# Strassen blocks of an up projection: high parts as one 512-column matmul, halves summed on GpSimd

## The chip, the cores and the metric

The kernel runs on one core of a Trainium2 chip. The time is device microseconds of one execution; the median of several runs is given. A profile is taken in an execution of its own, whose span is given beside the median. TensorE (PE in the profile) multiplies matrices out of SBUF into PSUM, with weight loads (PEld) beside the matmuls; VectorE (DVE), ScalarE (ACT) and GpSimd (POOL) do the rest, each with a queue that is worked off in order; SyncE (SP) and GpSimd issue DMAs.

## What is computed

Two layers of an encoder on 512 tokens of 1024 features. The part that the change touches is the gated MLP at the end of each layer:

```python
hf = rms_norm(x, ffn_norm_g[l])
u = depthwise_conv(hf @ ffn_w_up[l], ffn_conv_w[l], ffn_conv_b[l])
u_gate, u_val = u[..., :D_FF], u[..., D_FF:]
x = x + (jax.nn.silu(u_gate) * u_val) @ ffn_w_down[l]
```

`D_FF` is 2816, so there are 22 column blocks of 128 for the gate and 22 for the value. The depthwise convolution has width 3, along the tokens. All inputs are float32.

## The kernel before

**High and low halves.** Every matmul operand is kept as two float32r tiles, a rounded high part and the rest as a low part, and every product is three matmuls: high by high, high by low, low by high (`mm3`, L534). A weight tile of 128x512 is split by `w_split` (L441) or, for the Strassen blocks, by `w_form` (L467). ScalarE rounds (`A.activation`, which the profile shows at L299). The low half is made in one of two ways: a subtraction on VectorE or GpSimd (L306), or `by_transfer` (L432), in which ScalarE writes minus the high part and a DMA issued by GpSimd adds the raw weight (L438).

**The order.** The whole program is written out by hand: a planner (`Clock`, L208) keeps a simulated time for each engine, adds the cost of every operation that is issued, and decides by it when the steps of a `chain` (L258) are put into the engines' queues. What is put in first runs first, whatever the real times are. `wnext` (L516) hands out weights in the order of `units` and lets the splits run 3, 4 or 6 units ahead. PSUM has eight banks under the tags `acc` (2), `S` (1), `ST` (2), `AV` (2) and `mi` (1).

**The up projection.** The first 4 column blocks of a layer are computed as they stand (`plain`, L1678). The other 18 use Strassen's scheme (the Winograd form): the two halves of the features, the gate and the value columns, and the two halves of the tokens make a 2x2 by 2x2 product of blocks, done in 7 products instead of 8 (`product`, L1693). Each product is 4 weight columns (`q`) with three matmuls of 256 tokens. `forms` holds, for each product and `q`, the high and low half of its token operand: slices of `HH` and `HL` for the products 11, 12 and 4, of a tile `tf` for the others. The sums of weight blocks that the products need are made in `w_form` on VectorE (tiles `raw` and `s`); the forms 11, 12 and 22 are plain blocks and take `by_transfer` (tiles `fh`, `fl`; all other split weights are `wh`, `wl`).

Products share banks: 11, 2, 3 add up in one of `acc`, 1 and 4 in one of `AV`, 12 and 22 have one of `ST` each. After a product its bank is either copied aside by ScalarE (`aside`, tile `sx`) or added by VectorE to an earlier copy (`add`, tile `u`), 256 columns each time. Then both 512-token results are multiplied by the norm factor `rbc` on VectorE (`scale`), and go through the convolution (`convolve`, L1656: one pass on ScalarE, two multiply-adds on VectorE, tile `a`), Silu, gate product and split into `ah`/`al` or `act`.

**The down projection.** The column blocks come in groups of 4, 5, 5, 5 and 3. The 8 output blocks of a finished group (`down`, L1765, three matmuls of 512 per column block) are dealt out between the products of the next group, after the products named in `SPOTS`, and added to the residual `XM` by VectorE. `_ffn` (L115) writes this order down.

Of the kernel before, what the change touches and what calls it, by code (L numbers as in the profile page):

```python
# [47 lines left out]
FORMS = ("11", "12", "1", "22", "2", "4", "3")  # L48
SPOTS = ("22", "2", "4", "3")
# [11 lines left out]
C_BIAS = 0.2  # L61

# [51 lines left out]

def _ffn():  # L115

    toks, late = [], []
    for g, (c0, c1) in enumerate(_groups()):  # L120
        dealt = len(late) - (KEEP * SIZES[g - 1] if g == len(SIZES) - 1 else 0)
        for n, c in enumerate(range(c0, c1)):
            if g == 0:
                toks += [("u", c, 0), ("u", c, 1)]
                continue
            now = late[:dealt * (n + 1) // (c1 - c0) - dealt * n // (c1 - c0)]
            late = late[len(now):]
            for f in FORMS:
                toks.append(("f", c, f))
                if f in SPOTS:  # L130
                    k = SPOTS.index(f)
                    toks += now[len(now) * k // len(SPOTS):len(now) * (k + 1) // len(SPOTS)]
        late += [("d", g, m, i) for m in range(KC) for i in range(c1 - c0)]
    return toks + late


def _layer_units():

    r = _widths()
    for tok in _ffn():  # L140
        if tok[0] == "u":
            r += [("u", T), ("p", T), ("next",)]
        elif tok[0] == "f":
            r.append(tok)
        elif (tok[2] * SIZES[tok[1]] + tok[3]) % 4 == 0:
            r.append(("u" if tok[1] < len(SIZES) - 1 else "p", T))
    return r
# [60 lines left out]
class Clock:  # L208
# [5 lines left out]
    def __init__(self):  # L214
        self.now, self.n, self.heap, self.busy = 0.0, 0, [], False
        self.fin, self.free, self.ready = 0.0, {}, {}
        self.source = self.last = None

# [39 lines left out]
    def chain(self, *steps, after=0.2):  # L258

        def go(n, source=None):  # L260
            if n == len(steps):
                return
            keys, fn = steps[n] if isinstance(steps[n], tuple) else ((), steps[n])
# [15 lines left out]
class Engine:  # L279
# [13 lines left out]
    def activation(self, out, in_, func, **k):  # L293
        t = self.TABLE.get(func)
        if t and t != self.table and not (t == 2 and func is AF.Tanh and self.table == 3):
            self.table = t
            self.ck.took(self.kind, 1.28)
        self._count(out, 0.00084, 0.09 + 0.09 * (len(k) > 0))
        return self.eng.activation(out, in_, func, **k)  # L299

    def _two(self, out, *a):
        self._count(out, *((0.14, 0.1) if ALU.pow in a else (0.002145, 0.127) if self.kind == "Pool" else (0.00105, 0.07)))
# [17 lines left out]
    def tensor_copy(self, out, in_, psum=False):  # L320
        self._count(out, 0.00105 if psum else 0.00053, 0.07)
        return self.eng.tensor_copy(out, in_)  # L322
# [15 lines left out]
def trunk(ctx: ExitStack, tc: tile.TileContext, x, w, prm, gb, cst, out):  # L338
# [44 lines left out]
    def soonest(*tags):  # L383

        for t in tags:
            while not banks[t]:
                ck.pop()
        return min(tags, key=lambda t: banks[t][0])
# [52 lines left out]
    def w_split():  # L441
# [9 lines left out]
        hi, lo = halves[j] = pair(j)  # L451
        ck.fin = ck.now
# [14 lines left out]
    def w_form(j, form, pi):  # L467
# [6 lines left out]
        if form in ("11", "12", "22"):  # L474
            hi, lo = halves[j] = pair(j, True)
            by_transfer(hi[:, :T], lo[:, :T], {"11": a11, "12": a12, "22": a22}[form])
            done("w", j)
            return
        hi, lo = halves[j] = pair(j)
        if form == "2":  # L480
# [5 lines left out]
            "4": (a12, a12, s2, ALU.subtract, [("sum", pi, "2")], None),  # L486
# [17 lines left out]
        chain((keys, total), lambda: A.activation(hi[:, :T], dst, AF.Copy), low, after=0.0)  # L504

    def pick(bias, t=0.0):

        t = max(t, ck.now)
        dve, pool = (max(t, ck.free.get(e, 0.0)) for e in ("DVE", "Pool"))
        return V if dve + 0.61 + bias < pool + 1.18 else G  # L510

# [13 lines left out]
    def mm(o, lhsT, rhs, start, stop, again=False):  # L525
        PE.matmul(o, lhsT=lhsT, rhs=rhs, start=start, stop=stop, skip_group_check=again)  # L526
        n = rhs.shape[-1]
        ck.to(ck.now + (n / 2400.0 + 0.0133 if st["ffn"] else max(0.107, n / 2370.0)))
# [12 lines left out]
    HH = cp.tile([P, KC, T], F32R, tag="HH", name="HH")  # L541
    HL = cp.tile([P, KC, T], F32R, tag="HL", name="HL")
# [140 lines left out]
    def layer(l, sq, xsrc):  # L683
# [904 lines left out]
        def build_forms(q):  # L1588
# [51 lines left out]
        st["ffn"] = True  # L1640
# [15 lines left out]
        def convolve(c, part, u):  # L1656
# [3 lines left out]
                lambda: A.activation(a[:, :T], u[:, :T], AF.Identity, bias=col(PRM_B + ci),  # L1660
                                     scale=col(PRM_W1 + ci)),
                lambda: V.scalar_tensor_tensor(a[:, 1:T], u[:, 0:T - 1], col(PRM_W0 + ci), a[:, 1:T],
                                               ALU.mult, ALU.add),
                lambda: V.scalar_tensor_tensor(a[:, 0:T - 1], u[:, 1:T], col(PRM_W2 + ci), a[:, 0:T - 1],
                                               ALU.mult, ALU.add)]
# [27 lines left out]
        def product(c, name):  # L1693

            if name == "11":
                quad["u"], quad["v"] = slot("u"), slot("u")
                quad["s"] = [slot("sx") for _ in range(2)]
                quad["a"] = ps("acc")
            if name in ("12", "1", "22"):
                quad[name] = ps({"12": "ST", "1": "AV", "22": "ST"}[name])  # L1700
            if name == "2":
                need(("s1", l, c))
            if name == "4":
                need(("s5", l, c))
            if name == "3":
                need(("s2", l, c))
            bank = quad[{"11": "a", "2": "a", "3": "a", "4": "1"}.get(name, name)]
            o = bank[:, 0:256]
# [6 lines left out]
            u, v, (sa, sb) = quad["u"], quad["v"], quad["s"]  # L1715
            lo, hi = slice(0, 256), slice(256, 512)

            def aside(dst, key, tag=None):
                def go():
                    A.activation(dst, o, AF.Copy)  # L1720
                    if tag:
                        free(tag)
                    done(key, l, c)
                chain(go)

            def add(dst, other, tag=None):
                def go():
                    V.tensor_tensor(dst, o, other, ALU.add)
# [3 lines left out]

            def scale(t):
                return [([("rbc", G2)], lambda: V.tensor_tensor(t[:, :T], t[:, :T], fin["rbc"][:, :T], ALU.mult))]

            if name == "11":
                aside(sa[:, lo], "s1")
            elif name == "12":
                chain(([("s1", l, c)], add(u[:, lo], sa[:, lo], "ST")))
            elif name == "1":  # L1740
                aside(sb[:, lo], "s5")
            elif name == "22":
                aside(sb[:, hi], "s4", "ST")
            elif name == "2":
                aside(sa[:, hi], "s2")
# [19 lines left out]
        def down(g, m, i):  # L1765
            c0, c1 = groups[g]
            n, kc, ends = c1 - c0, c0 + i, g == len(groups) - 1
            b = m * n + i
# [44 lines left out]
        st["ffn"] = False  # L1813
# [62 lines left out]
def _pack_weights(i):  # L1876
    res = []
    for l in range(L):
# [34 lines left out]
        for kind, *tok in _ffn():  # L1913
# [8 lines left out]
            elif kind == "d":  # L1922
                g, m, k = tok
                c0, c1 = _groups()[g]
                if (m * (c1 - c0) + k) % 4 == 0:
                    at = [divmod(m * (c1 - c0) + k + n, c1 - c0) for n in range(4)]
                    res.append(np.concatenate([dn[(c0 + k_) * P:(c0 + k_ + 1) * P, m_ * P:m_ * P + P]
                                               for m_, k_ in at], axis=1))
# [82 lines left out]
```

## Time and profile before

| | |
|---|---|
| median of 3 runs | 1542.81 us |
| lowest and highest | 1542.35, 1544.06 us |
| span of the profiled execution | 1542.9 us |
| weight packets, share of 16 DMA engines (q1, hardware) | 33.9% |
| DMAs that GpSimd issues (q0, software) | 29.6% |
| stage of the Strassen blocks, layer 0 | from 469.0 to 746.15 us |
| the same, layer 1 | from 1236.8 to 1514.2 us |

A group of instructions is given by source line, engine, operation, tiles (written <- read) and shape, with its count, then its busy time in us and the mean of one in ns, then the idle time of the engine before it and who ended it. A row of the timeline begins with start and duration in us; neighbours of one kind are merged, with their number behind the x. In a row of windows each engine has its busy time and, in brackets, its number of instructions; then follow the granted share of TensorE's clock, the share of the DMA engines and GB/s. Lines are those of helpers: all matmuls stand at L526, all ScalarE passes at L299, all two-input operations of VectorE and GpSimd at L306 and L310.

### The profile page before, as it was taken

What the parts mean: (1) busy time and instruction counts of PE and PEld (TensorE: products, weight loads), DVE (VectorE), ACT (ScalarE), POOL (GpSimd) and SP (SyncE); (2) the same over time, 40 slices, a digit from 0 to 9 for tenths busy, and PEclk for the clock granted to TensorE, in tenths of its full rate; (3) what the DMA queues carried; (4) which work ended last, traced back from release to release, by engine and by line L of the source; (5) the groups of instructions that cost most, each with busy time, mean ns of one, the idle gap of its engine ahead of it and who ended that gap; (6) DMA issues with size and microseconds to landing.
All of it is one profiled execution on the core that took longest, in us unless ns stands there. A gap on an engine that the chain in (4) does not pass through costs nothing.

```text
span 1542.9 us, 24572 instructions
## 1 busy us (share of the span) xinstructions
PE 1536.2 (100%) x8337; PEld 1342.9 (87%) x8337; DVE 1161.6 (75%) x1959; ACT 1076.8 (70%) x2014; POOL 766.8 (50%) x829
## 2 busy tenths in 40 slices
PE   9999999999999999999999999999999999999999
PEld 8888888888889999999898888888888899999997
DVE  6777886776688888888746688768666888888885
ACT  6557875877677877777554587758766677777772
POOL 2884886753452323222588648766435522222222
PEclk9999999999999999999999999999999999999999
DMA  7432344658978878777454323547498778788763
GB/s 238 112 118 83 89 124 142 163 128 204 233 177 191 181 185 187 192 176 153 139 148 127 117 76 86 139 141 168 110 220 216 193 181 190 179 186 193 177 140 109
DMA packets 140381, 243.36 MB, mean 158 GB/s; under 512 B 31072, under 2 KB 53600, under 8 KB 140256
## 3 DMA queue, kind: packets, MB, share of 16 engines
q1 hardware_dynamic: 91872, 162.93, 33.9%
q0 software_dynamic: 43488, 78.66, 29.6%
q8 instruction: 65, 1.06, 0.3%
q10 hardware_dynamic: 4896, 0.21, 0.2%
q14 instruction: 60, 0.49, 0.1%
HBM read 149.41 MB, written 13.63 MB: 106 GB/s over the span
## 4 chain that ended last, share of the span: by engine, by line
PE 98%; DMA 1%; ACT 0%; DVE 0%; issue 0%; SPq 0%; POOL 0%; ACTq 0%; DVEq 0%
PE ps_acc L526 42%; PE ps_AV L526 19%; PE ps_ST L526 17%; PE ps_S L526 10%; PE ps_mi L526 10%; DMA qa<-nm 0%; DMA XM<-x 0%; DVE ka L322 0%; POOL wl L306 0%; ACT wh L299 0%; PE ps_mi L531 0%; PE ps_S L531 0%; SPq L407 0%; SPq L1835 0%; DVE XM L310 0%
## 5 line engine op out<-in xcount | busy, mean ns | idle before, releaser
L438 POOL DMA_DIRECT2D wl<-raw x194 | 175.5, 911 | 408.3 <-ACT wl L299 184.4
L299 ACT ACTIVATE wh<-raw 128x512 fp32r<-128x512 f32 (+2 forms) x449 | 265.0, 605 | 58.6 <-DVE raw L306 13.7
L306 POOL TENSOR_TENSOR wl<-raw,wh 128x512 fp32r<-128x512 f32 (+2 forms) x164 | 205.5, 1262 | 144.8 <-ACT wh L299 139.2
L438 POOL DMA_DIRECT2D fl<-raw x108 | 94.2, 873 | 168.2 <-ACT fl L299 66.2
L526 PE MATMUL ps_acc<-HH,wh 128*128 128x512 f32 x400 | 156.8, 392 | 0.4 <-DVE XM L310 0.4
L526 PE MATMUL ps_acc<-HH,wl 128*128 128x512 f32 x400 | 156.4, 391 | 0.0
L526 PE MATMUL ps_acc<-HL,wh 128*128 128x512 f32 x400 | 156.4, 391 | 0.0
L310 DVE SCALAR_TENSOR_TENSOR a<-u,prm,a 128x511 f32<-128x511 f32 x176 | 134.7, 768 | 18.7 <-ACT a L299 18.1
L299 ACT ACTIVATE wl<-wh 128x512 fp32r<-128x512 f32 (+1 forms) x194 | 121.9, 628 | 6.1
L314 DVE TENSOR_REDUCE nm<-ps_S 128x1 fp32r<-128x512 f32 x128 | 87.9, 687 | 44.5 <-PE ps_S L526 43.9
L299 ACT ACTIVATE a<-u,prm 128x512 f32<-128x512 f32 x88 | 71.2, 812 | 56.1 <-DVE u L306 56.0
L526 PE MATMUL ps_acc<-tf,wh 128*128 128x256 f32 x576 | 106.2, 282 | 0.0
L526 PEld LDWEIGHTS ps_acc<-tf,wh 128*128 128x128 f32 x576 | 94.3, 191 | 6.0
L526 PEld LDWEIGHTS ps_acc<-HH,wl 128*128 128x128 f32 x400 | 75.1, 188 | 16.3
L526 PEld LDWEIGHTS ps_acc<-HH,wh 128*128 128x128 f32 x400 | 75.4, 189 | 15.4 <-issue 0.7
L526 PEld LDWEIGHTS ps_acc<-HL,wh 128*128 128x128 f32 x400 | 75.2, 188 | 15.4
L526 PE MATMUL ps_acc<-tf,wl 128*128 128x256 f32 x288 | 81.5, 283 | 0.0
L526 PE MATMUL ps_AV<-HH,wl 128*128 128x256 f32 (+1 forms) x240 | 78.2, 326 | 0.0
L526 PE MATMUL ps_AV<-HH,wh 128*128 128x256 f32 (+1 forms) x240 | 78.2, 326 | 0.0
L526 PE MATMUL ps_AV<-HL,wh 128*128 128x256 f32 (+1 forms) x240 | 78.2, 326 | 0.0
L306 DVE TENSOR_TENSOR wl<-raw,wh 128x512 fp32r<-128x512 f32 (+1 forms) x92 | 64.3, 699 | 16.3 <-ACT wh L299 16.0
L306 DVE TENSOR_TENSOR pl<-ps_ST,ph 128x512 fp32r<-128x512 f32 x86 | 58.4, 683 | 18.5 <-ACT ph L299 15.0
(427 smaller groups left out, 5035.3 us busy)
## 6 DMA issues: line engine op xcount, KB each, us to landing
raw<-w SPq DMA_DIRECT2D x153, 512.0 KB, 4.0
wl<-raw POOLq DMA_DIRECT2D x190, 256.0 KB, 4.1
raw<-w SPq DMA_DIRECT2D x151, 256.0 KB, 3.8
fl<-raw POOLq DMA_DIRECT2D x108, 256.0 KB, 5.0
raw<-w SPq DMA_DIRECT2D x13, 384.0 KB, 3.1
XM<-x SPq DMA_DIRECT2D x16, 256.0 KB, 4.5
dtq<-tr SPq DMA_DIRECT2D x16, 192.0 KB, 2.1
dtk<-tr SPq DMA_DIRECT2D x16, 192.0 KB, 3.2
```

The source lines that it names most:

```text
L299: return self.eng.activation(out, in_, func, **k)
L306: return self.eng.tensor_tensor(out, *a)
L310: return self.eng.scalar_tensor_tensor(out, *a)
L314: return self.eng.tensor_reduce(out, in_, *a, **k)
L438: nc.gpsimd.dma_start(f(lo), r, accum_op=ALU.add)
L526: PE.matmul(o, lhsT=lhsT, rhs=rhs, start=start, stop=stop, skip_group_check=again)
```

## The change

- The high and the low half of a token operand stand side by side: `HX` replaces `HH` and `HL`, and `forms` holds one view of [high|low], 2 x 256 columns (for 11, 12 and 4 two pieces apart in `HX`).
- A product's column is two matmuls: the high weight by [high|low] into all 512 columns of the bank, and the low weight by high into the right half. A product is then the sum of the two halves of its bank.
- Copies aside and adds are 512 wide, on tiles `s1`, `s2`, `s4`, `s5`. A copy goes to ScalarE or VectorE, whichever the planner has free first. The halves are summed afterwards by `fold` on GpSimd, four of 256 columns per block, and `scale` moves to GpSimd.
- In the whole MLP stage weights are split by ScalarE and a subtraction on GpSimd; `by_transfer` isn't used there. The low halves of the summed forms (1, 2, 4, 3) stay on VectorE.
- The products come in another order, and banks other than `acc` are taken by `soonest`. The first two spots of a group get no down products, and in the first two output blocks the last column block of the group comes after the others (`_downs`).
- The planner's costs in this stage change (`exact`), and some steps of a chain yield for a while to an engine that is taken in its simulated time (`W_ACT`, `W_DVE`, `U_ACT`, `U_DVE`).

```diff
-FORMS = ("11", "12", "1", "22", "2", "4", "3")
-SPOTS = ("22", "2", "4", "3")
+FORMS = ("11", "1", "12", "2", "4", "22", "3")
+SPOTS = ("12", "4", "22", "3")
+SKIP = 2
...
+def _downs(g):
+
+    n = SIZES[g]
+    first = [(m, i) for m in (0, 1) for i in range(n - 1)] + [(0, n - 1), (1, n - 1)]
+    return [("d", g, m, i, b) for b, (m, i) in enumerate(first + [(m, i) for m in range(2, KC) for i in range(n)])]
...
+            for engine, slack, most in yields:
+                since = self.now if since is None else since
+                wait = min(self.free.get(engine, 0.0) - slack, since + most) - self.now
+                if wait > 0.01:
+                    self.at(wait, lambda: go(n, None, since))
+                    return
...
@@ w_split @@
+        if st["ffn"]:
+            last = pi + 1 == len(pieces) or pieces[pi + 1][0] != sl
+
+            def low():
+                G.tensor_tensor(lo[:, :wd], r, f(hi[:, :wd]), ALU.subtract)
+                done("w", j)
+                if last:
+                    w_free(sl)
+
+            chain(((), lambda: A.activation(hi[:, :wd], r, AF.Copy), W_ACT), low, after=0.0)
+            return
...
@@ w_form @@
-            by_transfer(hi[:, :T], lo[:, :T], {"11": a11, "12": a12, "22": a22}[form])
-            done("w", j)
+            r = {"11": a11, "12": a12, "22": a22}[form]
+
+            def low():
+                G.tensor_tensor(lo[:, :T], r, f(hi[:, :T]), ALU.subtract)
+                done("w", j)
+                done("raw", pi, form)
+
+            chain(((), lambda: A.activation(hi[:, :T], r, AF.Copy), W_ACT), ((), low), after=0.0)
             return
...
-        chain((keys, total), lambda: A.activation(hi[:, :T], dst, AF.Copy), low, after=0.0)
+        chain((keys, total, W_DVE), ((), lambda: A.activation(hi[:, :T], dst, AF.Copy), W_ACT), ((), low, W_DVE), after=0.0)
...
-    HH = cp.tile([P, KC, T], F32R, tag="HH", name="HH")
-    HL = cp.tile([P, KC, T], F32R, tag="HL", name="HL")
+    HX = cp.tile([P, 2, KC, T], F32R, tag="HX", name="HX")
+    HH, HL = HX[:, 0], HX[:, 1]
...
-                forms[name, q] = d[:, lo], d[:, hi]
+                forms[name, q] = d.rearrange("p (n t) -> p n t", n=2)
...
-                forms[name, q] = HH[:, k, h], HL[:, k, h]
+                forms[name, q] = HX[:, :, k, h]
...
@@ product @@
-                ws, (dh, dl) = slice(q * P, q * P + P), forms[name, q]
-                mm3(o, wh[:, ws], wl[:, ws], dh, dl, q == 0 and name in ("11", "12", "1", "22"),
-                    q == 3, name not in ("12", "22"))
+                ws, d = slice(q * P, q * P + P), forms[name, q]
+                again = name not in ("12", "22")
+                mm(o.rearrange("p (n t) -> p n t", n=2), wh[:, ws], d, q == 0 and name in ("11", "12", "1", "22"),
+                   False, again)
+                mm(o[:, 256:512], wl[:, ws], d[:, 0], False, q == 3, again)
...
-                    A.activation(dst, o, AF.Copy)
+                    copy(s[n][:, :T], o)
...
-                    V.tensor_tensor(dst, o, other, ALU.add)
+                    V.tensor_tensor(s[n][:, :T], o, s[n][:, :T], ALU.add)
...
+            def fold(t, h, n):
+                return lambda: G.tensor_tensor(t[:, h], s[n][:, lo], s[n][:, hi], ALU.add)
+
             def scale(t):
-                return [([("rbc", G2)], lambda: V.tensor_tensor(t[:, :T], t[:, :T], fin["rbc"][:, :T], ALU.mult))]
+                return [([("rbc", G2)],
+                         lambda: G.tensor_tensor(t[:, :T], t[:, :T], fin["rbc"][:, :T], ALU.mult))]
...
-                chain(([("s1", l, c)], add(u[:, lo], sa[:, lo], "ST")))
+                chain(([("s1", l, c)], add("1", tag)), fold(s["1"], lo, "1"), lambda: done("u", l, c))
...
-                chain(([("s2", l, c)], add(u[:, hi], sa[:, hi], "AV")), *scale(u), *convolve(c, 0, u))
+                u = s["1"]
+                chain(([("s2", l, c)], add("2", tag)), ([("u", l, c)], fold(u, hi, "2")), *scale(u), *convolve(c, 0, u))
             else:
-                chain(([("s4", l, c)], add(v[:, hi], sb[:, lo])), add(v[:, lo], sb[:, hi], "acc"), *scale(v), *convolve(c, 1, v))
+                v = s["4"]
+                chain(([("s4", l, c)], add("4")), add("5", tag), fold(v, lo, "4"), fold(v, hi, "5"), *scale(v),
+                      *convolve(c, 1, v))
...
-                state["tag"] = tags[m % 3] if ends else ("mi", "S")[m % 2]
-                state["acc"] = ps(state["tag"])
-            acc, tag = state["acc"], state["tag"]
+                tag = tags[m % 3] if ends else soonest("mi", "S", "ST", "AV")
+                state["acc", m] = ps(tag), tag
+            acc, tag = state["acc", m]
```

More of the change, by code (lines that the diff above doesn't have):

```diff
@@ L61 @@
 C_BIAS = 0.2
+F_BIAS = 0.0
+W_ACT, W_DVE = ("ACT", 0.0, 2.0), ("DVE", 0.0, 2.0)
+U_ACT, U_DVE = ("ACT", 0.7, 1.0), ("DVE", 0.7, 1.0)
 PRM_AG, PRM_FG, PRM_PS, PRM_CQ, PRM_CKV = 0, 8, 16, 20, 22
@@ L121, in _ffn @@
         dealt = len(late) - (KEEP * SIZES[g - 1] if g == len(SIZES) - 1 else 0)
+        done = 0
         for n, c in enumerate(range(c0, c1)):
@@ L125, in _ffn @@
                 continue
-            now = late[:dealt * (n + 1) // (c1 - c0) - dealt * n // (c1 - c0)]
-            late = late[len(now):]
             for f in FORMS:
@@ L130, in _ffn @@
                 if f in SPOTS:
-                    k = SPOTS.index(f)
-                    toks += now[len(now) * k // len(SPOTS):len(now) * (k + 1) // len(SPOTS)]
-        late += [("d", g, m, i) for m in range(KC) for i in range(c1 - c0)]
+                    spots = len(SPOTS) * (c1 - c0) - SKIP
+                    k = max(0, len(SPOTS) * n + SPOTS.index(f) + 1 - SKIP)
+                    now = dealt * k // spots - done
+                    done += now
+                    toks += late[:now]
+                    late = late[now:]
+        late += _downs(g)
     return toks + late
@@ L258, in chain, with go @@
     def chain(self, *steps, after=0.2):
-        def go(n, source=None):
+        def go(n, source=None, since=None):
             if n == len(steps):
                 return
-            keys, fn = steps[n] if isinstance(steps[n], tuple) else ((), steps[n])
+            keys, fn, *yields = steps[n] if isinstance(steps[n], tuple) else ((), steps[n])
             late = [self.ready.get(k, self.now + 0.5) for k in keys]
@@ L383, in soonest @@
     def soonest(*tags):
[L385 to L388, printed above, removed]
+        while not any(banks[t] for t in tags):
+            ck.pop()
+        return min((t for t in tags if banks[t]), key=lambda t: banks[t][0])
     def free(tag):
@@ L485, in w_form @@
             "2": (s2, a21, a11, ALU.subtract, [("sum", pi, "1")], 0),
-            "4": (a12, a12, s2, ALU.subtract, [("sum", pi, "2")], None),
+            "4": (a12, a12, s2, ALU.subtract, [("sum", pi, "2"), ("raw", pi, "12")], None),
             "3": (s2, a22, s2, ALU.subtract, [("sum", pi, "4"), ("form", pi, "2")], 3)}[form]
@@ L510, in pick, with sooner @@
         return V if dve + 0.61 + bias < pool + 1.18 else G
+    def sooner(n):
+        dve, pool = (max(ck.now, ck.free.get(e, 0.0)) for e in ("DVE", "Pool"))
+        return V if dve + 0.16 + 0.00105 * n + F_BIAS < pool + 0.16 + 0.0022 * n else G
     def w_ahead(j):
@@ L1695, in product @@
             if name == "11":
-                quad["u"], quad["v"] = slot("u"), slot("u")
-                quad["s"] = [slot("sx") for _ in range(2)]
+                quad["s"] = {n: slot("s" + n) for n in ("1", "2", "4", "5")}
                 quad["a"] = ps("acc")
             if name in ("12", "1", "22"):
[L1700 to L1708, printed above, removed]
+                quad["t" + name] = soonest("ST", "AV", "mi", "S")
+                quad[name] = ps(quad["t" + name])
+            tag = quad["t1" if name == "4" else "t" + name] if name in ("12", "1", "22", "4") else "acc"
+            for first, key in (("2", "s1"), ("4", "s5"), ("3", "s2")):
+                if name == first:
+                    need((key, l, c))
+            o = quad[{"11": "a", "2": "a", "3": "a", "4": "1"}.get(name, name)]
             wh, wl = wnext()
@@ L1763, in out_half, with down @@
             (SY, nc.scalar)[n].dma_start(out[KC - 1][:, ts], XM[:, KC - 1, ts])
-        def down(g, m, i):
+        def down(g, m, i, b):
             c0, c1 = groups[g]
             n, kc, ends = c1 - c0, c0 + i, g == len(groups) - 1
-            b = m * n + i
             if b % 4 == 0:
@@ L1922, in _pack_weights @@
             elif kind == "d":
[L1923 to L1928, printed above, removed]
+                g, *_, b = tok
+                c0, _ = _groups()[g]
+                if b % 4 == 0:
+                    res.append(np.concatenate([dn[(c0 + k) * P:(c0 + k + 1) * P, m * P:m * P + P]
+                                               for _, _, m, k, _ in _downs(g)[b:b + 4]], axis=1))
     pieces, swidth, _, _ = _stream()
```

44 lines of the change are left out of this document (23 added, 21 removed).

## The prediction

> **What bounds the kernel now.** I read the page's first and fourth part, then the waits of TensorE, then the windows around the stage that the change rewrites, cut at the first and the last 256-column matmul of each layer.
>
> ```profile
> span 1542.9 us, 24572 instructions
> PE 1536.2 (100%) x8337; PEld 1342.9 (87%) x8337; DVE 1161.6 (75%) x1959; ACT 1076.8 (70%) x2014; POOL 766.8 (50%) x829
> ...
> PEclk9999999999999999999999999999999999999999
> ...
> PE 98%; DMA 1%; ACT 0%; DVE 0%; issue 0%; SPq 0%; POOL 0%; ACTq 0%; DVEq 0%
> ```
> ```profile
> PE ps_ST L526 <- DMA qa<-nm: 1.5, 1, 1.5
> ```
> ```profile
> core 0: us, PE busy (x) PEld busy (x) DVE busy (x) ACT busy (x) POOL busy (x), PEclk, DMA share, GB/s
> 469.00:746.15 277.15, 277.15 (x1930) 259.39 (x1928) 226.44 (x384) 210.06 (x392) 76.30 (x88) 1.00 0.78 175
> 1236.80:1514.20 277.40, 277.40 (x1930) 259.44 (x1929) 226.44 (x384) 210.08 (x392) 76.34 (x88) 1.00 0.78 175
> ```
> TensorE is the whole chain and waits for almost nobody: its longest wait in the execution is 1.5 us. So the time before is TensorE's own issue rate. The two Strassen stages last 277.15 + 277.40 = 554.55 us; in them VectorE is busy for 82% (226.44 of 277.15), and GpSimd for 28%, all of it issuing DMAs, as the next rows show. Sums are made against the 1542.9 us of this execution; the median of the runs is 1542.81, so no correction is needed.
>
> **The change, TensorE's part.** A block is 7 products of 4 weight columns with 3 matmuls each, 84 of 256 columns; 18 blocks in each of 2 layers make 3024. Afterwards each column has one matmul of 512 and one of 256: the same columns, 1008 matmuls fewer.
>
> ```profile
> 420.02 0.39 PE L526 MATMUL ps_ST<-mgl,wh 128*128 128x512 f32 x1
> 420.25 0.39 PE L526 MATMUL ps_ST<-mgh,wl 128*128 128x512 f32 x1
> ...
> 420.93 0.39 PE L526 MATMUL ps_ST<-mgh,wl 128*128 128x512 f32 x1
> ```
> ```profile
> 488.61 0.40 PE L526 MATMUL ps_ST<-tf,fh 128*128 128x256 f32 x2
> 488.85 0.28 PE L526 MATMUL ps_ST<-tf,fl 128*128 128x256 f32 x1
> 488.97 0.63 PE L526 MATMUL ps_S<-act,wh 128*128 128x512 f32 x2
> 489.44 0.39 PE L526 MATMUL ps_S<-act,wl 128*128 128x512 f32 x1
> 489.67 0.40 PE L526 MATMUL ps_acc<-tf,wh 128*128 128x256 f32 x2
> ```
> Here starts count, not durations, since matmuls overlap. Three of 256 take 488.97 - 488.61 = 0.36 us, 0.120 each. Four steps of 512 take 420.93 - 420.02 = 0.91, 0.227 each; beside 256s three take 489.67 - 488.97 = 0.70, 0.233 each. A column now costs 0.360 and afterwards 0.227 + 0.120 = 0.347, or 0.353 with the slower 512: **13 ns less, 1008 times, 13.1 us** (7 us with 0.353). No row shows 512 and 256 alternating, nor a moving operand in two strided pieces (the products 11, 12 and 4); I bound the gain by nothing and by twice the figure, and take 13 us, from the nearest rows.
> The Trainium skill ("TensorE: Matmul & The Clock Gate", Back-to-back issue gap) puts the fixed part of a warm matmul at about 2.5 ns, so that fusing would bring 1008 x 2.5 ns, an estimate of 2.5 us; the rows show 13 ns and decide.
>
> **The change, the other engines.** Three weights of a block and every down weight had their low half made by ScalarE and an accumulating DMA, which goes; GpSimd now subtracts. Evacuations become 512 wide; the halves are folded by GpSimd (four 256-wide adds), which also takes the two multiplications by the norm factor from VectorE.
>
> ```profile
> L438 POOL DMA_DIRECT2D fl<-raw x51 | 44.1, 865 | 79.3 <-ACT fl L299 28.1 <-DVE a L310 20.8 <-ACT sx L299 17.5
> L438 POOL DMA_DIRECT2D wl<-raw x37 | 32.2, 870 | 121.4 <-ACT sx L299 69.2 <-ACT wl L299 33.3 <-DVE u L306 6.2
> ```
> ```profile
> L310 DVE SCALAR_TENSOR_TENSOR a<-u,prm,a 128x511 f32<-128x511 f32 x72 | 53.8, 747 | 6.3 <-ACT a L299 6.1
> L306 DVE TENSOR_TENSOR wl<-s,wh 128x512 fp32r<-128x512 f32 x36 | 24.7, 685 | 0.3 <-PE ps_AV L526 0.2
> L306 DVE TENSOR_TENSOR u<-u,rbc 128x512 f32<-128x512 f32 x35 | 24.2, 690 | 0.8
> ...
> L306 DVE TENSOR_TENSOR u<-ps_acc,sx 128x256 f32<-128x256 f32 x34 | 14.1, 418 | 0.0
> ```
> These are groups of layer 0's stage (the trailing figures are idle time). GpSimd gets, per stage, 54 form weights (18 x 3), 37 down weights and 36 multiplications, 127 operations of 512, and 72 folds. VectorE loses 24.2 us and has 72 adds that take 0.69 instead of 0.42 (19 us): some 221 us. ScalarE drops a pass for each of 5 weights a block and has four wider copies: under its 210. By busy time alone all would fit under 270 us. But the operands meet:
>
> ```profile
> 47.22 1.43 DVE L306 TENSOR_TENSOR mxl<-win,mxh 128x512 fp32r<-128x512 f32 x1 [2.00 <-ACT mxh L299]
> ```
> ```profile
> 45.80 1.04 POOL L306 TENSOR_TENSOR win<-pp 128x518 f32<-128x518 f32 x1
> 46.81 1.29 POOL L306 TENSOR_TENSOR wl<-raw,wh 128x512 fp32r<-128x512 f32 x1
> 48.06 1.49 POOL L306 TENSOR_TENSOR win<-win 128x516 f32<-128x516 f32 x1
> ```
> ```profile
> 768.18 2.71 DVE L310 SCALAR_TENSOR_TENSOR HL<-XM,prm,HH 128x512 fp32r<-128x512 f32 x2
> ```
> ```profile
> 767.62 1.02 POOL L306 TENSOR_TENSOR wl<-raw,wh 128x384 fp32r<-128x384 f32 x1
> 768.60 1.75 POOL L306 TENSOR_TENSOR sq<-sq,sqt 128x512 f32<-128x512 f32 x1
> 770.30 1.47 POOL L306 TENSOR_TENSOR wl<-raw,wh 128x384 fp32r<-128x384 f32 x1
> ```
> VectorE's subtraction of two SBUF tiles at 47.22 takes 1.43 us instead of 0.69: it runs only when GpSimd's operation of 46.81 is about done. GpSimd's next, at 48.06, takes 1.49 where its like took 1.04: it has waited for VectorE in turn. At 768 the two alternate: the 384-wide operation takes 1.02 free and 1.47 behind VectorE, 0.45 more, and one GpSimd operation of 512 with one of VectorE takes 770.30 - 768.60 = **1.70 us, which is 1.25 (48.06 - 46.81, GpSimd alone) plus 0.45**. Operations whose first input is PSUM are spared:
>
> ```profile
> 748.14 0.74 DVE L306 TENSOR_TENSOR u<-ps_acc,sx 128x256 f32<-128x256 f32 x2
> ```
> ```profile
> 746.33 3.04 POOL L306 TENSOR_TENSOR wl<-raw,wh 128x512 fp32r<-128x512 f32 x2 [1.74 <-ACT wh L299]
> ```
> Two such adds run at full speed inside GpSimd's pair. So GpSimd arithmetic and VectorE operations with two SBUF inputs exclude each other. The old Strassen stage has no GpSimd arithmetic and pays nothing; the new one is full of it.
>
> **The sum.** Per stage VectorE keeps 14 two-SBUF operations per block (4 form sums, 4 low halves, 4 convolution steps, gate product, low half of the activation): 252.
>
> ```profile
> 485.43 0.69 DVE L306 TENSOR_TENSOR u<-u,rbc 128x512 f32<-128x512 f32 x1
> 486.03 0.69 DVE L306 TENSOR_TENSOR s<-raw,s 128x512 f32<-128x512 f32 x1
> ```
> ```profile
> L306 POOL TENSOR_TENSOR wl<-raw,wh 128x256 fp32r<-128x256 f32 x4 | 3.0, 740 | 11.2 <-ACT wh L299 11.2
> ```
> GpSimd: 127 x 1.25 = 159 us; 72 folds at 0.70 (0.74 less the 0.04 by which neighbours overlap) = 50, together 209. VectorE: 252 x 0.45 = 113 if each slips between two of GpSimd's, 252 x 0.60 (486.03 - 485.43) = 151 if they come in blocks. The sum is 322 to 360 us per stage, where TensorE needs 277.3 - 6.5 = 270.8. A fold reads two halves of one tile and may go at the 1.04/1.29 of such a pair at 45.80, 10 us less: 312. I take **343**, the middle of 326 (199 operations alternating, 53 behind one another: 209 + 90 + 32 = 331, less half of those 10) and 360, since no in-order pair keeps the pair of inputs busy all the time. That is 343 - 277.3 = 65.7 us more per stage, 131.4 in all: 1542.9 + 131.4 = 1674.3, **1675 us** in round figures. TensorE's 13 us vanish in its new waits.
>
> The delay reaches TensorE so: a VectorE operation that is held up has the PSUM adds queued behind it, so banks come free late; a fold that waits for such an add has low halves of weights behind it on GpSimd, and the next product needs them. The weights are made at most 6 units ahead, some 10 us, which covers single waits and not a lasting deficit. The new order of products, the bank that is free soonest, the shared tile of halves and the new order of the down products I cost at nothing: they move no work, and a TensorE that waits anyway hides them. At the end of a stage the last activation comes through longer steps (adds and folds 0.7 each, 1.25 for the factor) behind 14 down products, 14 x 0.70 = 9.8 us; that may cost 0 to 5 us per layer, in the range.
>
> **Rivals.**
> - *The inputs are held for whole durations.* 127 x 1.29 + 72 x 0.74 + 180 x 0.69 + 72 x 0.747 = 395 us per stage, 118 more: 1778. The 0.45 speaks against it. Long TensorE gaps that lower its clock would end near there too; the clock row of the page stays at 9 (90% or more) all along, through the wait of 1.5 us too. Beyond 1745: 6%. The Trainium skill ("SBUF — State Buffer", SBUF: two separate sides) says that whichever of the two starts first holds the shared ports for its whole instruction. The rows agree on the exclusion, not on its length: VectorE adds 0.45 to GpSimd, not its 0.69. By that rule the stage would come to the 395 us of this rival.
> - *The deficit is partly absorbed*, because the folds are short and the schedule keeps the two apart, with GpSimd working during VectorE's PSUM operations and copies: the stage stays under 313 us, between 1550 and 1615. 5%.
> - *TensorE stays the bound, and it gets faster.* This needs GpSimd's arithmetic to fall from 209 us per stage to below 157 (270.8 less VectorE's 113); then 1542.9 - 13.1 = 1530. For it: busy sums alone fit, and the old stage had slack. Against it: none of the held-up pairs above overlapped. 8%.
> - *The fused matmul brings nothing* and TensorE is still the bound: 1543. 1%.
>
> **How the numbers follow.** The forecast has 80%: 1675, with 1615 (313 us per stage) to 1745 (360 with 5% idle, 378). That is the range. A measurement here can tell about 0.2%, 3 us, from no change. Faster 8%, same 1%, slower 91%.
>
> **What would show it.** Right: in the Strassen stages VectorE's two-SBUF operations average 0.9 to 1.2 us instead of 0.69, GpSimd's of 512 more than 1.4 instead of 1.29, PSUM adds stay at 0.69; TensorE shows waits for GpSimd's and VectorE's low halves; each stage lasts 330 to 360 us. The step of TensorE shows apart: 512 then 256 start to start in 0.347 us where nothing waits. Wrong: stages of 271 us, no TensorE waits, and VectorE's 0.69 unchanged beside GpSimd arithmetic; or stages that are long with those durations unchanged, which would put the delay in queue order instead of the ports.

## The result and the profile after

The changed kernel takes 1719.79 us (median of 4 runs, 1719.20 to 1719.89) against 1543.43 us of the kernel before beside it: a ratio of 1.1138, with a 95% interval of 1.1123 to 1.1154. The profiled execution has a span of 1717.2 us, 174.3 more than before.

First the page of the changed kernel: busy time of each engine, then the chain that ended last.

```profile
span 1717.2 us, 22171 instructions
PE 1589.4 (93%) x7329; PEld 1320.3 (77%) x7329; DVE 1397.6 (81%) x1880; ACT 996.5 (58%) x1824; POOL 1188.5 (69%) x1046
...
PE 2%; issue 0%; DVE 0%; POOL 0%; ACT 0%; POOLq 0%; ACTq 0%
```
The 1008 matmuls are gone (8337 to 7329). The chain, 98% TensorE before, breaks off after 2% and says nothing about the rest. The windows of the two Strassen stages, cut as before at their first and last 256-column matmul, show where the time went:

```profile
470.00:824.30 354.30, 299.23 (x1425) 244.21 (x1424) 344.39 (x357) 172.67 (x299) 276.88 (x193) 0.94 0.24 72
...
1323.70:1679.30 355.60, 303.42 (x1426) 248.44 (x1426) 345.67 (x358) 172.96 (x300) 276.27 (x193) 0.92 0.23 72
```
The stages take 709.9 us instead of 554.55, which is 155.35 of the 174.3. VectorE is busy for 344.39 of the 354.30 us of the first, 97%, while GpSimd (276.88) has 77 us to spare. The groups of VectorE in layer 0's stage say what it is busy with:

```profile
L332 DVE SCALAR_TENSOR_TENSOR a<-s,prm,a 128x511 f32<-128x511 f32 x68 | 79.3, 1167 | 7.2 <-ACT a L321 6.7
L328 DVE TENSOR_TENSOR wl<-raw,wh 128x512 fp32r<-128x512 f32 x35 | 44.0, 1258 | 0.2
L328 DVE TENSOR_TENSOR wl<-s,wh 128x512 fp32r<-128x512 f32 x36 | 40.2, 1116 | 1.8 <-ACT wh L321 1.0
...
L328 DVE TENSOR_TENSOR s<-ps_acc,s 128x512 f32<-128x512 f32 x34 | 22.7, 678 | 0.0
```
The operations with two SBUF inputs rose from 747 and 685 ns to 1167, 1258 and 1116; the adds out of PSUM stand at 678. The waiting lies inside the durations, so a waiting VectorE counts as busy. GpSimd's groups in the same stretch have grown as well, from 1.29 us for 512 columns and 0.74 for 256:

```profile
L328 POOL TENSOR_TENSOR fl<-raw,fh 128x512 fp32r<-128x512 f32 x52 | 86.1, 1659 | 29.2 <-ACT fh L321 28.6 <-DVE raw L328 0.6
L328 POOL TENSOR_TENSOR s<-s 128x256 f32<-128x256 f32 x69 | 76.3, 1106 | 31.1 <-DVE s L328 29.4 <-PE ps_S L569 1.2
```
The timelines, of VectorE and then of GpSimd, show the alternation itself (start, duration):

```profile
599.98 1.23 DVE L328 TENSOR_TENSOR wl<-raw,wh 128x512 fp32r<-128x512 f32 x1
601.13 1.78 DVE L328 TENSOR_TENSOR s<-raw,raw 128x512 f32<-128x512 f32 x1
602.83 1.78 DVE L328 TENSOR_TENSOR act<-a,act 128x512 fp32r<-128x512 f32 x1
```
```profile
600.62 1.74 POOL L328 TENSOR_TENSOR fl<-raw,fh 128x512 fp32r<-128x512 f32 x1
602.32 1.74 POOL L328 TENSOR_TENSOR s<-s,rbc 128x512 f32<-128x512 f32 x1
```
From 600.62 to 602.32 one GpSimd operation and one of VectorE take 1.70 us, the same as in the trace before. TensorE's waits name who was late:

```profile
PE ps_acc L569 <- ACT s L321: 51.2, 22, 4.3
PE ps_acc L569 <- DVE wl L328: 18.5, 15, 2.5
PE ps_AV L569 <- DVE wl L328: 15.5, 6, 5.6
PE ps_acc L569 <- ACT act L321: 13.8, 2, 7.0
```
Low halves come late from VectorE. So do the copies aside on ScalarE: they stand in its queue behind passes that wait for VectorE, most often Silu (`a<-a`), which needs the multiply-adds of the convolution, or the rounding of a weight sum (`wh<-raw`, `wh<-s`). ScalarE's timeline ahead of one such wait, in which TensorE stood for 3.75 us until 570.90, shows both (in brackets the idle time before, and who ended it):

```profile
568.13 0.63 ACT L321 ACTIVATE a<-a 128x512 f32<-128x512 f32 x1 [1.49 <-DVE a L332]
569.74 0.63 ACT L321 ACTIVATE wh<-raw 128x512 fp32r<-128x512 f32 x1 [0.98 <-DVE raw L328]
570.27 0.58 ACT L321 ACTIVATE s<-ps_acc 128x512 f32<-128x512 f32 x1
```
The last of TensorE's waits (`act`) lies outside the stages: at the end of each the last activation is some 7 us late.

### The profile page after: what moved, and what is told of

It reads as the page before. It is cut to its first block, busy times and chain, and to the rows that moved or that the text cites. A ratio compares the mean times of both kernels' runs of the same rounds, so it can differ in the third digit from the quotient of the medians.

```text
span 1717.2 us, 22171 instructions
## 1 busy us (share of the span) xinstructions
PE 1589.4 (93%) x7329; PEld 1320.3 (77%) x7329; DVE 1397.6 (81%) x1880; ACT 996.5 (58%) x1824; POOL 1188.5 (69%) x1046
## 5 line engine op out<-in xcount | busy, mean ns | idle before, releaser
L328 POOL TENSOR_TENSOR wl<-raw,wh 128x512 fp32r<-128x512 f32 (+2 forms) x253 | 349.9, 1390 | 187.8 <-ACT wh L321 173.8
L569 PE MATMUL ps_acc<-HX,wh 128*128 128x512 f32 x800 | 248.1, 391 | 0.4 <-DVE XM L332 0.4
L328 POOL TENSOR_TENSOR fl<-raw,fh 128x512 fp32r<-128x512 f32 x108 | 177.7, 1649 | 62.3 <-ACT fh L321 61.0
L328 POOL TENSOR_TENSOR s<-s 128x256 f32<-128x256 f32 x144 | 157.7, 1096 | 63.6 <-DVE s L328 61.4
L332 DVE SCALAR_TENSOR_TENSOR a<-s,prm,a 128x511 f32<-128x511 f32 x144 | 166.9, 1159 | 31.4 <-ACT a L321 30.2
L569 PEld LDWEIGHTS ps_acc<-HX,wh 128*128 128x128 f32 x800 | 150.0, 188 | 31.9 <-issue 0.7
L569 PE MATMUL ps_acc<-tf,wh 128*128 128x512 f32 x288 | 120.2, 443 | 51.2 <-ACT s L321 51.2
L569 PE MATMUL ps_acc<-HX,wl 128*128 128x512 f32 x400 | 156.4, 391 | 0.0
L328 POOL TENSOR_TENSOR s<-s,rbc 128x512 f32<-128x512 f32 x72 | 117.5, 1632 | 3.0
L328 DVE TENSOR_TENSOR wl<-s,wh 128x512 fp32r<-128x512 f32 x72 | 80.3, 1116 | 3.6 <-ACT wh L321 2.0
```

The source lines that it names most:

```text
L328: return self.eng.tensor_tensor(out, *a)
L332: return self.eng.scalar_tensor_tensor(out, *a)
```

## The experiments

All times are medians, or one run where the table says so, beside runs of the kernel before on the same chip (1543.3 to 1544.4 us). "Stage" is layer 0's Strassen stage and "VectorE" its busy time in it. "Waits" is the part of that busy time which exceeds the own work of the same operations (225.2 us by e2, 226.4 in the old order); it is left empty where no run shows the own work.

| run | us | ratio (95%) | stage | VectorE | waits |
|---|---|---|---|---|---|
| before | 1543.4 | 1 | 277.2 | 226.4 | 0 |
| changed | 1719.8 | 1.1123 to 1.1154 | 354.3 | 344.4 | 119 |
| e2, GpSimd only fills | 1536.9 | one run | 272.8 | 225.2 | 0 |
| e1, transfers | 1677.2 | 1.0852 to 1.0888 | 337.5 | 317.0 | |
| e3, scale on VectorE | 1699.1 | one run | 347.9 | 343.8 | |
| e4, both | 1621.1 | 1.0481 to 1.0512 | 311.0 | 294.2 | |
| e5, no GpSimd arithmetic | 1588.2 | 1.0273 to 1.0304 | 300.7 | 272.8 | 0 |
| e6, low halves alone | 1634.5 | 1.0574 to 1.0606 | 322.0 | 305.7 | 79 |
| e7, only folds read | 1560.6 | one run | 284.2 | 274.9 | 50 |
| e8, more transfers | 1652.5 | 1.0695 to 1.0736 | 330.3 | 267.4 | 0 |
| e9, plain DMA issues | 1571.7 | one run | 290.0 | 280.4 | 55 |
| e12, accumulating issues | 1609.0 | one run | 304.5 | 290.2 | 65 |
| e10, VectorE relieved | 1578.3 | 1.0199 to 1.0242 | 293.6 | 259.7 | 0 |
| e11, with other costs | 1569.6 | 1.0149 to 1.0179 | 290.4 | 264.3 | 0 |

**Does reading matter, or GpSimd's time and the order?** In e2 GpSimd's arithmetic of the stage is replaced, in place, by fills.

```diff
     def tensor_tensor(self, out, *a):
         self._two(out, *a)
+        if self.kind == "Pool" and self.ck.exact:
+            plain = out.bitcast(F32)
+            self.eng.memset(plain, 1.0)
+            return self.eng.memset(plain, 0.0)
```


> The changed kernel, with every GpSimd addition, subtraction and multiplication of the MLP stage replaced by two fills of the same tile, so that GpSimd is busy for about as long (1.03 us for 512 columns, by the fills of 1x512) and in the same place of every queue, and reads nothing; low halves, folds and norm factor are left out of the computation. Theory A: without the reads nothing excludes VectorE; its operations go back to 0.69, and the kernel takes 1528 to 1560. Theory B (order and GpSimd's time): the order is the same and the time nearly so, 1640 or more. A third reading, that GpSimd's writes hold VectorE up as well, also gives 1640 or more, but with VectorE's operations still at 1.1 to 1.3 us.

1536.92 us. The windows of its stages, and two groups of the first:

```profile
469.60:742.40 272.80, 272.80 (x1425) 232.24 (x1424) 225.17 (x351) 171.35 (x296) 164.73 (x386) 1.00 0.30 95
1232.50:1505.30 272.80, 272.80 (x1425) 232.27 (x1424) 225.15 (x351) 171.25 (x296) 164.74 (x386) 1.00 0.30 95
```
```profile
L331 POOL MEMSET fl<- 128x512 f32 x50 | 26.3, 527 | 2.9
```
```profile
L332 DVE TENSOR_TENSOR wl<-s,wh 128x512 fp32r<-128x512 f32 x35 | 23.9, 684 | 2.1 <-ACT wh L321 2.1
```
GpSimd is busy for 165 us, all queues are in the changed kernel's order, TensorE is busy throughout the stages and VectorE's operations are back at 684 ns. So the slowdown isn't in the order, nor in GpSimd's writes: it goes with the arithmetic that reads. Whether the reading or the computing does it, no run separates. Two things came along: the two fills of 527 ns are shorter than the 1.29 us of the operation that they replace, and a fill doesn't wait for ScalarE's high half, so GpSimd could start earlier than in the changed kernel.

**Taking the reads away by halves.** e1 gives the plain forms and the down weights back to the transfers; e3 moves the multiplications back to VectorE; e4 does both.

```diff
@@ w_form, and likewise w_split @@
-            def low():
-                G.tensor_tensor(lo[:, :T], r, f(hi[:, :T]), ALU.subtract)
...
+            by_transfer(hi[:, :T], lo[:, :T], r)
+            done("w", j)
+            done("raw", pi, form)
+            return
@@ scale (e3, e4) @@
-                         lambda: G.tensor_tensor(t[:, :T], t[:, :T], fin["rbc"][:, :T], ALU.mult))]
+                         lambda: V.tensor_tensor(t[:, :T], t[:, :T], fin["rbc"][:, :T], ALU.mult))]
```


> The changed kernel, with the low halves of the plain forms (11, 12, 22) and of the down weights made by ScalarE and an accumulating DMA again, as before the change; all else as changed, the fused matmul, the folds and the multiplications on GpSimd too. Theory A (GpSimd arithmetic and VectorE operations with two SBUF inputs exclude each other): GpSimd's arithmetic falls from 209 to about 95 us a stage, with VectorE's 113 to 151 that is 208 to 246, under TensorE's 271: both stages shrink to 271 to 285 us and the kernel takes 1528 to 1560, faster than before the change if nothing else waits. Theory B (the order of the queues, the yields and the longer chains delay TensorE, whatever the ports do): they are all still there, so 1650 or more. Theory C (the fused matmul is slow): the same, 1650 or more.

> The changed kernel with the 36 multiplications a layer by the norm factor back on VectorE. Theory A: GpSimd loses 45 us a stage and VectorE gains 36 two-SBUF operations, 16 to 22 us of the shared inputs: 23 to 29 us less a stage, 1660 to 1675 in all. Theory B, in the form that VectorE is simply too full: VectorE gets 36 x 0.6 = 22 us more work a stage, so about 1760.

> Both of the above: transfers for the plain forms and the down weights, the multiplications on VectorE, the folds on GpSimd. Theory A: GpSimd's arithmetic is 50 us a stage, VectorE's two-SBUF operations 130 to 173: 180 to 223 us, so TensorE is the bound, 1528 to 1545; VectorE's own work is about 245 of 271 us, so this may come out behind the run with the multiplications on GpSimd by some us. Theory B: 1650 or more.

1677, 1699 and 1621 us: each step down in GpSimd arithmetic is a step down in time, but all three lie above the sums, e3 by 24 us and e1 and e4 by far. By its number e1 even falls to the rival (the order, 1650 or more); e2, in the same order at 1537 us, speaks against that. In the sum I had added the two engines' holds and compared them with TensorE's 271 us. VectorE doesn't work like that: it stands in its queue while GpSimd holds the inputs, and its own work is still to be done. e1 also shows waits that the changed kernel doesn't have:

```profile
602.83 3.74 DVE L328 TENSOR_TENSOR wl<-raw,wh 128x512 fp32r<-128x512 f32 x1
```
```profile
601.53 0.88 POOL L459 DMA_DIRECT2D wl<-raw  x1 [2.92 <-ACT wl L321]
602.14 1.73 POOL L328 TENSOR_TENSOR s<-s 128x256 f32<-128x256 f32 x2
603.52 1.20 POOL L459 DMA_DIRECT2D fl<-raw  x1
604.13 1.89 POOL L328 TENSOR_TENSOR s<-s,rbc 128x512 f32<-128x512 f32 x1
```
The first row is VectorE's, the others GpSimd's. One subtraction of VectorE sits through the folds, a DMA issue and a multiplication, 3.74 us, with no turn in between.

**Is it the DMA issues?** e7 keeps e1's reads (folds and multiplications) and drops the issues: the subtractions become two fills. e9 makes that one fill and a plain DMA to a DRAM tile that nobody reads; in e12 this DMA accumulates.

```diff
+        if self.kind == "Pool" and self.ck.exact and ALU.subtract in a:
+            self.eng.memset(out.bitcast(F32), 0.0)
+            self.turn += 1
+            t = self.scratch[self.turn % len(self.scratch)]
+            return self.eng.dma_start(t[:, :a[0].shape[-1]], a[0], accum_op=ALU.add)
```
(e12; e9 without `accum_op`, e7 with a second fill instead of the DMA.)

> The changed kernel, in which GpSimd's subtractions in the MLP stage are replaced by two fills of the same tile (the low halves of those weights are left out of the computation), while the folds and the multiplications on GpSimd stay. GpSimd then reads as much as in the run with transfers (95 us a stage), but issues no DMA in the stage. If the waits depend on the arithmetic alone, it comes out like that run, stages of about 338 us and 1675 in all. If a DMA issue just ahead of GpSimd arithmetic is what made VectorE's waits so long there (single waits of 2 to 3.7 us), VectorE needs 221 + 0.59 x 95 = 277 us a stage and the kernel takes 1535 to 1570.

> As the run in which only the folds and multiplications on GpSimd read, but each of the replaced subtractions is one fill followed by a DMA issued by GpSimd that copies the raw weight to a DRAM tile that nobody reads; the low halves are left out of the computation. GpSimd reads as before (95 us a stage), nobody waits for the DMAs, and some 89 DMA issues of 0.87 us a stage stand in GpSimd's queue between the folds. If a DMA issue just ahead of GpSimd arithmetic is what lengthens VectorE's waits, single waits of 2 us and more come back, VectorE is busy for 300 us and more a stage and the kernel takes 1600 to 1680. If the long waits of the run with transfers came from the transfers' landings or from the order alone, it stays at 1550 to 1575.

> The run before with DMA issues beside the folds, the DMA now an accumulating one (still into a DRAM tile that nobody reads; the low halves are left out). In the run with transfers an issue took 0.92 us and a fold behind it never less than 1.02; with plain copies an issue took 0.56 and a fold behind it 0.73 at least. If it is the accumulating issue that lengthens the folds and VectorE's waits, issues go to 0.87 or more, folds behind them to 1.02 or more, waits of over 1.85 us become as many as in the run with transfers (46 after the attention of layer 0), and the kernel takes 1590 to 1660. If not, 1565 to 1580, and what made the run with transfers slow lies in its landings or its order.

1560.6, 1571.7, 1609.0 us, one run each. Plain issues cost 11 us; accumulating ones 37 more. GpSimd's timeline of e9 and then of e12, and last VectorE's of e12:

```profile
584.42 0.56 POOL L334 DMA_DIRECT2D scr<-raw  x1
585.00 1.30 POOL L335 TENSOR_TENSOR s<-s,rbc 128x512 f32<-128x512 f32 x1
586.26 0.74 POOL L335 TENSOR_TENSOR s<-s 128x256 f32<-128x256 f32 x1
```
```profile
590.10 0.88 POOL L334 DMA_DIRECT2D scr<-raw  x1
590.71 1.59 POOL L335 TENSOR_TENSOR s<-s,rbc 128x512 f32<-128x512 f32 x1
591.97 1.02 POOL L335 TENSOR_TENSOR s<-s 128x256 f32<-128x256 f32 x1
```
```profile
590.81 2.74 DVE L335 TENSOR_TENSOR wl<-s,wh 128x512 fp32r<-128x512 f32 x1
```
An accumulating issue takes 0.88 instead of 0.56, the operation behind it 1.59 instead of 1.30, and VectorE (last row) waits through both that follow. GpSimd itself isn't slower: from the issue to the multiplication 0.61 us pass instead of 0.58, and from that to the fold 1.26 in both runs. What has grown is the overlap: each operation still lasts for some 0.3 us after the next one has started, where it was 0.04 at most, and VectorE finds no gap. In the two Strassen stages VectorE has 13 operations of over 1.85 us in e9, 30 in e12, 42 in e1, one in the changed kernel and none in e7. Not all of the 37 us is this: in layer 0's stage VectorE's busy time grows by 10 us from e9 to e12 and the stage by 15, and VectorE stands idle for 4.5 us, against 0.6, until a DMA has read `raw`. So a good part of e1's surplus over e7, 48 of 117 us, comes with the issues; the rest stays open (in e1 ScalarE is fuller by a pass per weight, and VectorE takes over more of the copies).

**Each part alone.** e5 has the fused matmul without any GpSimd arithmetic in the stage: e4, with the folds on VectorE (`V.tensor_tensor` in `fold`). e6 is the kernel before with the low halves on GpSimd alone:

```diff
@@ before: w_split and w_form @@
-            by_transfer(hi[:, :T], lo[:, :T], {"11": a11, "12": a12, "22": a22}[form])
+            r = {"11": a11, "12": a12, "22": a22}[form]
+            A.activation(hi[:, :T], r, AF.Copy)
+            G.tensor_tensor(lo[:, :T], r, f(hi[:, :T]), ALU.subtract)
```


> The fused matmul alone: transfers for the plain forms and the down weights, the folds and the multiplications by the norm factor on VectorE, so that GpSimd does no arithmetic in the MLP stage. Theory A (GpSimd arithmetic and VectorE operations with two SBUF inputs exclude each other): VectorE's operations are back at 0.69 us; its own work is about 265 us a stage beside TensorE's 272.8 (as measured with the fills), so 1535 to 1555, with some waits because VectorE has almost no slack. Theory B (the new order and the longer chains cost the time): 1600 or more, since nothing of the order has changed.

> The kernel before the change with one part of it alone: in the MLP stage all weights but those of the summed forms get their low half by a subtraction on GpSimd; the 256-column matmuls, 256-wide evacuations and VectorE's multiplications stay. Theory A: GpSimd has some 91 x 1.25 = 114 us of arithmetic a stage and VectorE's own work is 226 us; if VectorE waits for 0.59 us of each us of GpSimd arithmetic, as in the changed kernel ((344 - 221) / 209), it needs 293 us a stage instead of TensorE's 277: about 1575, 1555 to 1600. Theory B: the old order and the old chains, shorter by the landing of a DMA, so no change, 1540 to 1548.

e6: 1634.5 us, above the 1555 to 1600 that I expected. Half of the slowdown comes with the old order of products and the old matmuls, so this half at least needs neither of the new ones. VectorE's waits are larger than I had taken, 79 us (305.7 less 226.4) for 90 operations, 0.88 each, against 0.62 in the changed kernel (119 for 193, where folds are among them). e5: 1588 us, not 1535 to 1555. The windows of layer 0, e5 first:

```profile
469.00:769.70 300.70, 283.59 (x1424) 237.31 (x1423) 272.77 (x469) 218.68 (x373) 77.12 (x89) 0.97 0.75 164
```
```profile
470.10:792.10 322.00, 291.95 (x1930) 266.43 (x1929) 305.70 (x390) 161.78 (x307) 137.52 (x90) 0.96 0.26 81
```
In e5 VectorE's operations are at 0.69 us again, but they sum to 272.8 us, as much as TensorE needs by e2; I had counted 265. Without GpSimd VectorE has hardly any room for the wider adds, the folds and the factor.

**Relieving VectorE.** e8 makes the low halves of the forms 1 and 4 by transfer too; e10, from e5, puts all copies on ScalarE and the low half of most activations on a transfer; e11 is e10 with another VectorE cost in the planner.

```diff
@@ e8, w_form @@
+        if form in ("1", "4"):
+            chain((keys, total, W_DVE), ((), moved, W_ACT), after=0.0)
+            return
@@ e10 @@
-                    copy(s[n][:, :T], o)
+                    A.activation(s[n][:, :T], o, AF.Copy)
...
... within the last step of convolve ...
-*split(ah, al, a[:, :T])
+*(split(ah, al, a[:, :T]) if c >= groups[-2][0] + 3 else [lambda: by_transfer(ah, al, a[:, :T])])
@@ e11, within the costs of _two @@
-(0.00104, 0.157) if self.ck.exact
+(0.00104, 0.07) if self.ck.exact
```
(`moved` is `by_transfer` of the weight sum.)

> As the fused matmul alone, and the low halves of the forms 1 and 4 are made by transfers too, so that VectorE loses 36 operations (22 us) a stage and ScalarE gains 36 passes of 0.63 us. Theory A: VectorE's own work is about 243 us and ScalarE's about 240 of 272.8 us: TensorE is the bound, 1533 to 1540, below the kernel before the change by 3 to 10 us. Theory B: 1600 or more.

> The fused matmul without GpSimd arithmetic, with VectorE relieved: all copies aside on ScalarE (24 x 0.6 = 14 us a stage), the low half of the activations of all but the last blocks by a transfer (some 10 us). VectorE's own work falls from 273 to about 249 us a stage, ScalarE's rises from 219 to about 243, TensorE needs 272.8. If VectorE's load alone set the time of the run without GpSimd arithmetic (stages of 300 us), stages of 275 to 285 us and 1540 to 1565 in all. If the order of the queues sets it, 1580 to 1600 again.

> The same with one constant of the planner changed: a VectorE operation of 512 costs 0.60 us in its simulated time, as the trace has them back to back, instead of 0.69. Only the order in the queues changes. If the order has a share in the waits that are left, some 5 to 20 us below the run without it; if VectorE's load is all, within 5 us of it.

e8 missed by far, 1652 us, with a new wait in place of the old one:

```profile
PE ps_AV L564 <- DMA wl<-raw: 42.9, 12, 7.5
PE ps_ST L564 <- DMA wl<-raw: 23.8, 8, 4.2
```
Sum, two passes on ScalarE and a transfer: TensorE waits up to 7.5 us for the landing. e10 and e11 come to 1578 and 1570 us, with VectorE at 260 and 264 us in stages of 294 and 290. Less load helped by 10 us, where VectorE's load as the only cause would have given 23 or more (1540 to 1565); e10 lies just under the range for the order of the queues (1580 to 1600). The planner's cost helped by another 9, within the 5 to 20 of a share of the order. So the order has a share. How much of the rest is VectorE's load, and what else holds e10 and e11 up with no engine full, wasn't settled. No version with the fused matmul that computes everything beat the kernel before; e2's 1537 us is what the matmuls could give, and it leaves part of the computation out.

## Why the prediction was right

**The cause, the sign and the range held.** The time fell inside the range (1615 to 1745), 45 us above the 1675. GpSimd's arithmetic and VectorE's operations with two SBUF inputs exclude each other: e2 shows that it goes with the arithmetic that reads, e6 that the new order isn't needed for it, and most of the rows predicted for it appeared: VectorE's operations with two SBUF inputs average 1.18 us in layer 0's stage (298 us for 252), GpSimd's of 512 take 1.65 and more, PSUM adds 0.68, and TensorE waits for VectorE's low halves.

**One link of the path didn't appear.** I had TensorE waiting for low halves that stand on GpSimd behind a late fold. For GpSimd's low halves it waited for 0.7 us in all; for VectorE's it was 48 us, and for the copies aside on ScalarE, which I hadn't named, 55 us.

**The term that was mis-sized** is the sum per stage, 343 us; it measured 354.3 and 355.6. I had taken the pair of inputs as the bound, nearly always in use. GpSimd in fact had 77 us idle: the bound was VectorE's queue, its own 225 us (e2) plus 119 of waiting, 97% of the stage. That a sum of the wrong things came within 4% is luck: each GpSimd operation happened to cost VectorE 0.62 us of waiting on average. Where the two ways of counting differ, in e1 and e4, the sum failed outright: it gave 208 to 246 and 180 to 223 us, under TensorE's 271, and the stages took 338 and 311. In the changed kernel the two stages make 24 of the 43 us by which the span exceeds the 1674.3.

**The rest lies outside the stages**: 174.3 - 155.35 = 19 us. The last activation cost two waits of 7 us, where I had said 0 to 5 per layer and put nothing into the sum; the other 5 were not followed.

**TensorE's step** was 13 ns a column and 13.1 us in all. e2, where nothing waits, has stages of 272.8 us instead of 277.2 and 277.4: 9.0 us less, 8.9 ns a column. Its timeline shows four columns of product 11, which is one of the strided ones:

```profile
601.42 0.39 PE L573 MATMUL ps_acc<-HX,fh 128*128 128x512 f32 x1
601.65 0.28 PE L573 MATMUL ps_acc<-HX,fl 128*128 128x256 f32 x1
...
602.83 0.40 PE L573 MATMUL ps_ST<-tf,wh 128*128 128x512 f32 x1
```
(602.83 - 601.42) / 4 = 0.353 us: the slower of the two figures that I had, 0.233 + 0.120, was the right one. The strides cost nothing that can be seen: in the changed kernel four columns that aren't strided (product 22, 819.44 to 820.84) take 0.350 each. The 2.5 us in all that I had worked out, as an estimate, from the fixed part of 2.5 ns in the Trainium skill ("TensorE: Matmul & The Clock Gate", Back-to-back issue gap) stay too low.

**The rivals.** "Held for whole durations" (1778) fell: one GpSimd and one VectorE operation took 1.70 us, not 1.29 + 0.69. Its companion, TensorE's clock, did come: the granted clock was 0.94 and 0.92 in the stages, with waits of up to 5.6 us, and TensorE was busy for 299 us in layer 0's where e2 has 273. What that adds to the stages wasn't separated; since VectorE's queue is idle for only 10 of the 354 us, little room is left for it. "TensorE stays the bound" would have ended at 1537 instead of 1530, as e2 has it. "Partly absorbed" fell with 354 us. What I had costed at nothing (order of products, banks, down products, the shared tile) cost nothing that shows in e2.

## What to carry to other kernels

Busy shares don't tell whether work may move to GpSimd: count VectorE's operations with two SBUF inputs beside it, and look in the trace for pairs of the two engines that overlap. If they wait for each other there, add to VectorE's own work what it will wait (here 0.5 to 0.9 us for each GpSimd operation, by the table's waits) and compare that, not the sum of the holds, with the bound engine. Here VectorE's adds with an input in PSUM (0.68 us) and GpSimd's fills, which only write (e2), were free of it.

## What the runs showed of the hardware that was not expected

After an accumulating DMA that GpSimd issues, its operations overlap: the trace has 0.88 us for the issue and 1.59 us for a 512-column multiplication behind it, against 0.56 and 1.30 with a plain DMA (e12, e9), while the distances from start to start stay the same (0.61 and 1.26 us against 0.58 and 1.26). So GpSimd keeps its pace, but VectorE waits through a whole run of its operations, 2.74 us in e12 and 3.74 in e1, where it otherwise gets its turn after each (1.78 us in the changed kernel). That the overlap is what denies it the turn is read from the timelines; it was not tried apart.
